# Sparse attention's score masks: from matrix products on the tensor engine to the vector engine's pass over the scores

## The chip, the cores and the metric

The kernel runs on one core of a Trainium2 chip. The metric is the device time of one launch in microseconds (us). The core has a tensor engine (PE; its weight loads are listed apart as PEld), a vector engine (DVE), a scalar engine (ACT), GpSimd (POOL) and a sync engine (SP) whose queue issues the DMAs here. Each engine takes its own instructions in order and waits for others by semaphores. Matrix products read SBUF and write PSUM; DVE and ACT read both.

## The reference, cut to what matters

The program is one decoder layer of 1024 tokens and width 1024: a common input projection, sparse attention with three branches (compressed, selected, window), gated linear attention, a gated merge, an output projection and a feed-forward block. The change touches the selected and the window branch. There are 2 key groups with 4 heads each, a head dimension of 64, and 8 query blocks of 128 tokens. With 16 selected blocks of 64 keys out of 16, the selected branch covers all earlier keys; the window is 512 wide.

```
sw = einsum('bghqd,bgkd->bghqk', q_pos, kwin)
m_w = (kpos >= 0) & (dist >= 0) & (dist < WINDOW)
p_w = softmax(where(m_w, sw, -1e30)) * m_w
o_w = einsum('bghqk,bgkd->bghqd', p_w, vwin)
```

So of the key blocks that one query block looks at, the last one (the diagonal) needs a lower triangle as its mask, and in a full window the first one (the edge) needs the opposite triangle. All the blocks between are unmasked.

## The kernel before

**Stages.** The input projection and the compressed keys come first, then gated linear attention (to about 340 us), then sparse attention (about 366 to 763 us), the merge, the output projection, and the feed-forward block. Products in full precision are made of three products of rounded 32-bit parts: lines L427, L1483 to L1485 and L1871 to L1873.

**Attention's units.** A unit is a group g and a query block i: `units` runs through (0, 7) down to (0, 0) and then (1, 0) up to (1, 7). A unit has five branches: the compressed one (`br` 0), and the selected (`br` 1) and the window one (`br` 2) for each of two head pairs j. A branch that looks at `nkb` key blocks has scores of w = 128 * nkb columns for each of its two heads. Up to four key blocks both heads share one score tile and one pass ("pair", `pair_scores`, query blocks 0 to 3, 32 passes in all). With more, each head has its own ("head", `head_scores`, query blocks 4 to 7, 64 passes in all; 40 of them 640 wide).

**One pass.** `products` puts the scores into a PSUM tile s (two such tiles exist): for each part of at most 512 columns a product with the high part of the queries (L1122) and one with the low part (L1123). Then masks are added by products with a 16-bit identity as weights: `meb` for the edge (L1125, when br is 2 and i is at least 4) and `mdb` for the diagonal (L1127, always). DVE reduces the scores to their negated maximum nm (L1150 for a pair, L1163 for a head), ACT computes exp(s + nm) from PSUM into a tile p in SBUF and sums it into z (L1153, L1165; the sum is read out by a second instruction), DVE inverts z (L1133), and the two heads are scaled, one on DVE (L1141), the other on ACT (L1139). Then p is transposed on PE (L1201), split into two parts (ACT L1178, DVE L1179) and multiplied with the values (L1210). There are four p buffers.

**What sets the order.** PE's order is the program's. `Plan` walks through the scores, the transposes ("turns") and the value products with estimated costs for PE, DVE, ACT and POOL, and wherever the next of these is over 300 ns away it issues one dense product from a queue named `fill` (14 gate and 5 up projections, L427, into the PSUM tile d). What is left of the queue after the last branch is flushed there. `score_at` gives no scores for a branch before the p buffer that they will use has been given back, and `turn` gives it back after the last transposes of its branch. The other engines' orders come from the framework's scheduler. SP issues all loads and stores in the order in which they stand in its queue.

**The queries' rooms.** Gated linear attention uses two constant tiles `QZ` (name qz, 128 x 512 values of 32 bits), in which the two heads' queries lie in halves padded with zeros. They are filled by L833, read by PE (L870) and by DVE (L849), and unused once its last chunk is done.

**Constants.** One array `consts` holds the identity, the masks and others by column; `load_consts` copies `mdb` and `meb` to 16-bit tiles at the start, from one load of 768 columns.

Of the kernel before, what the change touches and what calls it, by code (L numbers as in the profile page):

```python
# [12 lines left out]
BF = mybir.dt.bfloat16  # L13
U8 = mybir.dt.uint8
AF = mybir.ActivationFunctionType
OP = mybir.AluOpType
# [14 lines left out]

CI, CTRI, CMD, CME, CCMP, CMUL, CLEV = 0, 128, 256, 384, 512, 1024, 1088
NCONST = CLEV + 64 * NLV


def constants():
    c = np.zeros((128, NCONST), np.float32)
    r = np.arange(128)[:, None]  # L40
    j = np.arange(128)[None, :]
    c[:, CI:CI + 128] = r == j
    c[:, CTRI:CTRI + 128] = (r <= j) / 16.0
    c[:, CMD:CMD + 128] = np.where(j <= r, 0.0, NEG)
    c[:, CME:CME + 128] = np.where(j > r, 0.0, NEG)
    n = np.arange(64)[None, None, :]
    t = np.arange(NB)[None, :, None] * 128 + np.arange(128)[:, None, None]
    ok = (n * CSTRIDE + CLEN - 1 <= t) & (n < NCMP)
    c[:, CCMP:CCMP + 512] = np.where(ok, 0.0, NEG).reshape(128, 512)
    c[:, CMUL:CMUL + 64] = ok[:, 0]  # L50
    for i, h in enumerate(LEVELS):
        q = np.arange(64)[None, :]
        c[:, CLEV + 64 * i:CLEV + 64 * (i + 1)] = (r // (2 * h) == q // h) & (r % (2 * h) < h)
    return c


def rope_tables():
# [51 lines left out]
class Plan:  # L109
# [52 lines left out]
    def score(self):  # L162
        b, fn, n = self.scores.popleft()
        fn()
        w = 64 if b.br == 0 else 128 * b.nkb
        if b.br == 0:
            cost = 540.0
        else:
            cost = n * (2 * max(107.0, w / 2.4) + 55.0 * (1 + (b.br == 2 and b.i >= 4)))
        self.t += cost  # L170
        self.s.pop(0)
        pf = self.p.pop(0) if b.br else 0.0
        m = n if b.br else 4
        t = self.on("D", self.t, 65 + 1.041 * w * m)
        t = self.on("A", max(t, pf), m * (237 + 0.833 * w))
        self.s.append(t + LAT)
        self.s.sort()
        t = self.on("D", t, 150.0)
        t = max(self.on("D", t, 130 + 0.52 * w if b.br else 330.0), self.on("A", t, 187 + 0.833 * w) if b.br and n == 2 else 0.0)
        b.ready = max(b.ready or 0.0, t + LAT)  # L180
        b.left = getattr(b, "left", 2) - n
# [58 lines left out]
def layer_kernel(ctx, tc, a, outT):  # L240
# [79 lines left out]
    onesr = cst.tile([128, 128], F32R, name="onesr")  # L320
    meanr = mcst.tile([128, 128], F32R, name="meanr")
    identb = mcst.tile([128, 128], BF, name="identb")
    mdb = mcst.tile([128, 128], BF, name="mdb")
    meb = mcst.tile([128, 128], BF, name="meb")
    cmb = mcst.tile([128, NB, 64], BF, name="cmb")
    lev = mcst.tile([128, NLV, 64], U8, name="lev")
    gains = cst.tile([128, 3, NK], F32, name="gains")
# [4 lines left out]
    def load_consts():  # L332
        load(ident, a["consts"][:, CI:CI + 128])
        load(tri, a["consts"][:, CTRI:CTRI + 128])
        load(cmul, a["consts"][:, CMUL:CMUL + 64])
        load(ggain, a["gla_norm"])
        load(w2b, a["gla_w2b"])
        V.tensor_copy(identb, ident)
        t = big("cst1")
        load(t[:, :768], a["consts"][:, CMD:CMD + 768])  # L340
        V.tensor_copy(mdb, t[:, 0:128])
        V.tensor_copy(meb, t[:, 128:256])
        V.tensor_copy(cmb.rearrange("p b n -> p (b n)"), t[:, 256:768])
        t = big("cst2")
        load(t[:, :64 * NLV], a["consts"][:, CLEV:CLEV + 64 * NLV])
        V.tensor_copy(lev.rearrange("p b n -> p (b n)"), t[:, :64 * NLV])
# [684 lines left out]


    psum("pp2", s=2, t=2, o=1, d=1)
    oa = [[None, None], [None, None]]
    spare = deque([ps_d])

# [39 lines left out]
    class Branch:  # L1076
# [37 lines left out]
        def products(self, par, s, w, parts):  # L1114
            d = UN[self.g, self.i]
            kk = ks[self.br - 1][self.g]
            edge = self.br == 2 and self.i >= 4
            for o, n in parts:
                dst = s[:, o:o + n]
                kv = kk[:, 128 * self.k0 + o:128 * self.k0 + o + n]  # L1120
                end = o + n == w
                PE.matmul(dst, d["qs"][par][:, 0, self.j, :], kv, start=True, stop=False)  # L1122
                PE.matmul(dst, d["qs"][par][:, 1, self.j, :], kv, start=False, stop=not end and not (edge and o == 0))  # L1123
                if edge and o == 0:
                    PE.matmul(s[:, 0:128], identb, meb, start=False, stop=not end)  # L1125
                if end:
                    PE.matmul(s[:, w - 128:w], identb, mdb, start=False, stop=True)  # L1127

        def weigh(self, pars, ps, z):

# [12 lines left out]
        def pair_scores(self):  # L1143
# [3 lines left out]
            for par in range(2):  # L1147
                self.products(par, s[:, par, :], w, [(0, w)])
            nm, z = tiny("nm", 2, 6), tiny("z", 2, 6)
            V.tensor_reduce(nm, s, AX, OP.max, negate=True)  # L1150
            p = prob("p", shape=(2, 512))[:, :, :w]
            for par in range(2):
                S.activation(p[:, par, :], s[:, par, :], AF.Exp, bias=nm[:, par:par + 1],  # L1153
                             accum_out=z[:, par:par + 1])
            self.weigh((0, 1), [p[:, 0, :], p[:, 1, :]], z)

        def head_scores(self, par):
# [2 lines left out]
            s = ps_s()[:, 512 - c:512 - c + w]  # L1160
            self.products(par, s, w, [(0, c), (c, w - c)][:1 if c == w else 2])
            nm, z = tiny("nm", 2, 6)[:, :1], tiny("z", 2, 6)[:, :1]
            V.tensor_reduce(nm, s, AX, OP.max, negate=True)  # L1163
            p = prob("p")[:, :w]
            S.activation(p, s, AF.Exp, bias=nm, accum_out=z)  # L1165
            self.weigh((par,), [p], z)

        def turns(self):
# [773 lines left out]
```

## Time and profile before

| what | value |
|---|---|
| median of 3 runs | 1574.86 us (1574.77 to 1575.18) |
| span of the profiled execution | 1571.8 us |
| median less the span | 3.1 us |
| instructions | 23022 |
| sparse attention, by its score passes | 366 to 756 us |
| diagonal mask products (L1127), edge mask products (L1125) | 128, 32 |
| granted TensorE clock, mean | 0.999 |

The profiled execution's own time is not listed beside its span; what lies around the span is taken as 3.1 us, the distance to the median. A row of the timeline gives an instruction's start, its duration, engine, line, and what it writes and reads. Products overlap on PE, and their ends are modelled, so durations on PE add up to more than the time they take: what a product costs is read from the distance between starts. "Busy" in the table of stretches is the union of the durations.

### The profile page before, as it was taken

The numbers are of one execution on the slowest core, as the hardware profiler recorded it, in microseconds if no ns is written. First come the engines' busy times: TensorE is split into PE (matmuls) and PEld (weight loads), VectorE is DVE, ScalarE is ACT, GpSimd is POOL, SyncE is SP. The second block draws the span as 40 slices with busy tenths as digits, with TensorE's granted clock in tenths as the row PEclk, the third lists the DMA queues.
The fourth block names the chain that finished last, engine by engine and source line by source line (L and its number), as shares of the span: only waits on it lengthen the run. The fifth ranks groups of instructions, "written<-read, shape, count | busy, mean of one in ns | idle before, by whom it ended". The sixth has DMA issues, their size and how long they took to land.

```text
span 1571.8 us, 23022 instructions
## 1 busy us (share of the span) xinstructions
PE 1556.8 (99%) x8031; PEld 1310.1 (83%) x8031; DVE 1014.1 (65%) x1630; ACT 810.0 (52%) x1615; POOL 719.7 (46%) x635
## 2 busy tenths in 40 slices
PE   9999999999999999999999999999999999999998
PEld 7888988888888888888888888888888888888887
DVE  7780487686777687667574577644444444499785
ACT  6241555575676686677654454334433334454542
POOL 6110466563223353253256520666666666555570
PEclk9999999999999999999999999999999999999999
DMA  5431112232111221131656622323222222795422
GB/s 180 140 104 62 61 55 79 97 107 81 45 51 57 71 83 56 51 109 60 205 184 211 215 83 81 114 101 106 102 101 101 101 101 101 282 340 161 141 88 107
DMA packets 109656, 179.86 MB, mean 114 GB/s; under 512 B 13394, under 2 KB 30435, under 8 KB 109540
## 3 DMA queue, kind: packets, MB, share of 16 engines
q1 hardware_dynamic: 105508, 171.96, 32.5%
q10 hardware_dynamic: 4032, 6.44, 1.1%
q8 instruction: 63, 1.03, 0.3%
q14 instruction: 53, 0.43, 0.1%
HBM read 128.27 MB, written 45.88 MB: 111 GB/s over the span
## 4 chain that ended last, share of the span: by engine, by line
PE 93%; DVE 4%; ACT 1%; issue 1%; DMA 1%; POOL 0%; SPq 0%; DVEq 0%; ACTq 0%; POOLq 0%
PE m L427 19%; PE d L427 10%; PE m L1484 9%; PE m L1485 9%; PE m L1483 9%; PE m L1873 4%; PE m L1871 4%; PE m L1872 4%; PE o L1210 4%; PE t L1201 3%; PE s L1122 2%; PE s L1123 2%; PE t L745 2%; PE t L747 1%; PE t L746 1%; PE t L880 1%
## 5 line engine op out<-in xcount | busy, mean ns | idle before, releaser
L369 POOL TENSOR_TENSOR wl<-wf,wh 128x512 fp32r<-128x512 f32 x106 | 146.3, 1385 | 275.6 <-ACT wh L368 274.8
L1484 PE MATMUL m<-xt,wh 128*128 128x512 f32 x412 | 160.3, 389 | 0.0
L1483 PE MATMUL m<-xt,wh 128*128 128x512 f32 x412 | 160.3, 389 | 0.0
L1485 PE MATMUL m<-xt,wl 128*128 128x512 f32 x412 | 160.3, 389 | 0.0
L1400 POOL TENSOR_TENSOR wl<-ws,wh 128x512 fp32r<-128x512 f32 x76 | 107.5, 1419 | 73.6 <-ACT wh L1399 73.6
L1400 POOL TENSOR_TENSOR wl<-wr,wh 128x512 fp32r<-128x512 f32 x69 | 92.0, 1333 | 70.0 <-ACT wh L1399 70.0
L1179 DVE TENSOR_TENSOR ptl<-t,pth 128x512 fp32r<-128x512 f32 (+1 forms) x168 | 99.5, 596 | 34.4 <-ACT pth L1178 31.4
L1399 ACT ACTIVATE wh<-wr 128x512 fp32r<-128x512 f32 x87 | 55.0, 632 | 121.0 <-POOL wl L1400 90.4
L1399 ACT ACTIVATE wh<-ws 128x512 fp32r<-128x512 f32 x76 | 48.0, 632 | 131.7 <-PE m L1484 112.6
L1178 ACT ACTIVATE pth<-t 128x512 fp32r<-128x512 f32 (+1 forms) x168 | 87.8, 524 | 53.2 <-PE t L1201 45.5
L1871 PE MATMUL m<-xb,wh 128*128 128x512 f32 x280 | 109.1, 389 | 0.3 <-DVE g L1545 0.3
L1400 POOL TENSOR_TENSOR wl<-wd,wh 128x512 fp32r<-128x512 f32 x56 | 82.1, 1468 | 58.9 <-ACT wh L1399 58.7
L1872 PE MATMUL m<-xb,wh 128*128 128x512 f32 x280 | 109.0, 389 | 0.0
L1873 PE MATMUL m<-xb,wl 128*128 128x512 f32 x280 | 108.9, 389 | 0.0
L1400 DVE TENSOR_TENSOR xb<-ar,xb 128x512 fp32r<-128x512 f32 x73 | 82.5, 1150 | 28.8 <-ACT xb L1399 28.8
L368 ACT ACTIVATE wh<-wf 128x512 fp32r<-128x512 f32 x106 | 66.2, 627 | 67.5 <-PE m L427 19.7
L427 PE MATMUL m<-hh,wh 128*128 128x512 f32 x240 | 99.9, 416 | 0.0
L427 PE MATMUL m<-hh,wl 128*128 128x512 f32 x240 | 93.8, 391 | 0.0
L427 PE MATMUL m<-hl,wh 128*128 128x512 f32 x240 | 93.6, 390 | 0.0
L1483 PEld LDWEIGHTS m<-xt,wh 128*128 128x128 f32 x412 | 77.4, 188 | 16.2
L1484 PEld LDWEIGHTS m<-xt,wh 128*128 128x128 f32 x412 | 77.4, 188 | 16.0
L1485 PEld LDWEIGHTS m<-xt,wl 128*128 128x128 f32 x412 | 77.4, 188 | 16.0
(422 smaller groups left out, 4569.4 us busy)
## 6 DMA issues: line engine op xcount, KB each, us to landing
ar<-actd SPq DMA_DIRECT2D x77, 256.0 KB, 3.0
wf<-in_w_t SPq DMA_DIRECT2D x58, 256.0 KB, 2.7
wr<-in_w_gate SPq DMA_DIRECT2D x44, 256.0 KB, 2.7
wr<-in_w_upf SPq DMA_DIRECT2D x44, 256.0 KB, 2.6
wd<-in_w_down SPq DMA_DIRECT2D x33, 256.0 KB, 5.1
zd<-zt SPq DMA_DIRECT2D x32, 256.0 KB, 2.0
zz<-zd SPq DMA_DIRECT2D x16, 512.0 KB, 4.6
wf<-in_w_out SPq DMA_DIRECT2D x32, 256.0 KB, 3.3
```

The costliest lines, as they stand in the source:

```text
L369: P.tensor_tensor(tl, wf, f(th), OP.subtract)
L427: PE.matmul(st["p"], w, x, start=k + i == 0, stop=k == n - 1 and i == 2)
L1178: S.activation(th[:, :c], pt[:, :c], AF.Copy)
L1179: V.tensor_tensor(tl[:, :c], pt[:, :c], f(th[:, :c]), OP.subtract)
L1399: S.activation(th, src, AF.Copy)
L1400: eng.tensor_tensor(tl, src, f(th), OP.subtract)
L1483: PE.matmul(ps, wh[:, c], xh, start=first and k == 0, stop=False, skip_group_check=not first)
L1484: PE.matmul(ps, wh[:, c], xl, start=False, stop=False, skip_group_check=not first)
L1485: PE.matmul(ps, wl[:, c], xh, start=False, stop=k == MH - 1, skip_group_check=not first)
L1871: PE.matmul(dst, wh[:, c], xh, start=first and p == 0, stop=False, skip_group_check=not first)
L1872: PE.matmul(dst, wh[:, c], xl, start=False, stop=False, skip_group_check=not first)
L1873: PE.matmul(dst, wl[:, c], xh, start=False, stop=p == NP - 1, skip_group_check=not first)
```

## The change

The two mask products and their weight loads go. In their place DVE's pass over the scores adds a mask from SBUF while it reads the scores from PSUM, writes -(s + mask) to the tile p, and reduces it by a minimum, which gives the negated maximum as before. ACT then computes exp(-p + nm) in place in p, from SBUF in place of PSUM. The mask of a pass is as wide as its scores: 1024 columns of 16 bits with the diagonal triangle at the end (the last w of them are used), and 640 columns with both triangles for the full windows. They are loaded into the two `QZ` tiles, packed two values to a 32-bit word, after gated linear attention. A pair's pass becomes two, one for each head. In `Plan`, a mask no longer counts on PE, the DVE pass has 65 ns for each head in place of each pass and waits for the p buffer, and the score tile comes free after DVE's pass in place of ACT's.

```diff
-CI, CTRI, CMD, CME, CCMP, CMUL, CLEV = 0, 128, 256, 384, 512, 1024, 1088
-NCONST = CLEV + 64 * NLV
+CI, CTRI, CCMP, CMUL, CLEV = 0, 128, 256, 768, 832
+CMS = CLEV + 64 * NLV
+CMW = CMS + 512
+NCONST = CMW + 320
...
+    late, edge = np.where(j <= r, 0.0, NEG), np.where(j > r, 0.0, NEG)
+    c[:, CMS:CMS + 512] = halves(np.concatenate([np.zeros((128, 896)), late], 1))
+    c[:, CMW:CMW + 320] = halves(np.concatenate([edge, np.zeros((128, 384)), late], 1))
...
-            cost = n * (2 * max(107.0, w / 2.4) + 55.0 * (1 + (b.br == 2 and b.i >= 4)))
+            cost = n * 2 * max(107.0, w / 2.4)
...
-        t = self.on("D", self.t, 65 + 1.041 * w * m)
-        t = self.on("A", max(t, pf), m * (237 + 0.833 * w))
-        self.s.append(t + LAT)
+        t = self.on("D", max(self.t, pf), 65 * m + 1.041 * w * m)
+        u, t = t, self.on("A", t, m * (237 + 0.833 * w))
+        self.s.append((u if b.br else t) + LAT)
...
-        load(t[:, :768], a["consts"][:, CMD:CMD + 768])
-        V.tensor_copy(mdb, t[:, 0:128])
-        V.tensor_copy(meb, t[:, 128:256])
-        V.tensor_copy(cmb.rearrange("p b n -> p (b n)"), t[:, 256:768])
+        load(t[:, :512], a["consts"][:, CCMP:CCMP + 512])
+        V.tensor_copy(cmb.rearrange("p b n -> p (b n)"), t[:, :512])
...
     psum("pp2", s=2, t=2, o=1, d=1)
+    masks = []
+    for t, o, n in zip(QZ, (CMS, CMW), (512, 320)):
+        t = t.rearrange("p a b c -> p (a b c)")[:, :n]
+        SP.dma_start(t, a["consts"][:, o:o + n])
+        masks.append(t.bitcast(BF))
...
-                PE.matmul(dst, d["qs"][par][:, 1, self.j, :], kv, start=False, stop=not end and not (edge and o == 0))
-                if edge and o == 0:
-                    PE.matmul(s[:, 0:128], identb, meb, start=False, stop=not end)
-                if end:
-                    PE.matmul(s[:, w - 128:w], identb, mdb, start=False, stop=True)
+                PE.matmul(dst, d["qs"][par][:, 1, self.j, :], kv, start=False, stop=True)
+
+        def masked(self, p, s, w, nm):
+
+            m = masks[1] if self.br == 2 and self.i >= 4 else masks[0][:, 1024 - w:]
+            V.tensor_tensor_reduce(out=p, in0=s, in1=m, scale=-1.0, scalar=3.0e38, op0=OP.add, op1=OP.min, accum_out=nm)
...
             nm, z = tiny("nm", 2, 6), tiny("z", 2, 6)
-            V.tensor_reduce(nm, s, AX, OP.max, negate=True)
             p = prob("p", shape=(2, 512))[:, :, :w]
             for par in range(2):
-                S.activation(p[:, par, :], s[:, par, :], AF.Exp, bias=nm[:, par:par + 1],
+                self.masked(p[:, par, :], s[:, par, :], w, nm[:, par:par + 1])
+            for par in range(2):
+                S.activation(p[:, par, :], p[:, par, :], AF.Exp, scale=-1.0, bias=nm[:, par:par + 1],
                              accum_out=z[:, par:par + 1])
...
-            V.tensor_reduce(nm, s, AX, OP.max, negate=True)
             p = prob("p")[:, :w]
-            S.activation(p, s, AF.Exp, bias=nm, accum_out=z)
+            self.masked(p, s, w, nm)
+            S.activation(p, p, AF.Exp, scale=-1.0, bias=nm, accum_out=z)
```

Line numbers shift: L1122 and L1123 become L1129 and L1130, L1150 and L1163 become L1135, L427 becomes L431, L1201 and L1210 become L1210 and L1219, L1179 becomes L1188.

**PE, a head of a full window** (the first one, of unit (0, 7)): what stood there before, from the scores' first part to the next dense product:

```order
L1122 MATMUL s<-ks_920,qs 128x384
L1123 MATMUL s<-ks_920,qs 128x384
L1125 LDWEIGHTS identb
L1125 MATMUL s<-meb,identb 128x128
L1122 MATMUL s<-ks_920,qs 128x256
L1123 MATMUL s<-ks_920,qs 128x256
L1127 LDWEIGHTS identb
L1127 MATMUL s<-mdb,identb 128x128
L427 MATMUL d<-hl,wh 128x512
```

And the same head in the change:

```order
L1129 MATMUL s<-ks_916,qs 128x384
L1130 MATMUL s<-ks_916,qs 128x384
L1129 MATMUL s<-ks_916,qs 128x256
L1130 MATMUL s<-ks_916,qs 128x256
L431 MATMUL d<-hh,wl 128x512
```

Both masks and their loads of weights are gone, and the score products follow each other directly. In the whole program 160 such products go. Of these, 148 stood ahead of another rounded 32-bit product (L427, L1122, L1193, L1210), 12 ahead of a transpose (L1185, L1201).

**DVE, the pairs of unit (0, 3)** (512 columns for each head), before:

```order
L1179 TENSOR_TENSOR ptl<-t,pth 128x256
L1150 TENSOR_REDUCE nm<-s 128x2
L1179 TENSOR_TENSOR ptl<-t,pth 128x512
L1150 TENSOR_REDUCE nm<-s 128x2
L1133 RECIPROCAL rr<-z 128x2
```

And in the change, where qz is the mask in the queries' room:

```order
L1188 TENSOR_TENSOR ptl<-t,pth 128x256
L1135 ISA p,nm<-s,qz_1345 128x512
L1135 ISA nm 128x1
L1135 ISA p,nm<-s,qz_1345 128x512
L1135 ISA nm 128x1
L1188 TENSOR_TENSOR ptl<-t,pth 128x512
L1135 ISA p,nm<-s,qz_1345 128x512
L1135 ISA nm 128x1
L1135 ISA p,nm<-s,qz_1345 128x512
L1135 ISA nm 128x1
L1141 RECIPROCAL rr<-z 128x2
```

One reduction of a pair becomes four instructions: for each head the pass and a second instruction that writes out its minimum. A head's reduction becomes two.

**PE, the end of attention** (after the last value products), before:

```order
L1210 MATMUL o<-ptl,vs_1043 128x256
L1210 MATMUL o<-ptl,vs_1044 128x256
L1210 MATMUL o<-pth,vs_1044 128x256
L1210 MATMUL o<-ptl,vs_1044 128x256
L427 MATMUL t<-obh,wh 128x512
L427 MATMUL t<-obl,wh 128x512
L427 MATMUL t<-obh,wl 128x512
```

And in the change:

```order
L1219 MATMUL o<-ptl,vs_1039 128x256
L1219 MATMUL o<-ptl,vs_1040 128x256
L1219 MATMUL o<-pth,vs_1040 128x256
L1219 MATMUL o<-ptl,vs_1040 128x256
L431 MATMUL m<-obh,wh 128x512
L431 MATMUL m<-obl,wh 128x512
L431 MATMUL m<-obh,wl 128x512
```

Before, 36 dense products of the fill queue (12 into t, 12 into o, 12 into d) stood between the last value product and the merge's first product (into m). In the change none do: all of the queue is issued within attention. The largest move is between the compressed scores of unit (0, 0) and those of unit (1, 3) (L1102 before, L1111 in the change): 94 dense products stood there before, and 142 do in the change.

More of the change, by code (lines that the diff above doesn't have):

```diff
@@ L43, in constants @@
     c[:, CTRI:CTRI + 128] = (r <= j) / 16.0
-    c[:, CMD:CMD + 128] = np.where(j <= r, 0.0, NEG)
-    c[:, CME:CME + 128] = np.where(j > r, 0.0, NEG)
     n = np.arange(64)[None, None, :]
@@ L53, in constants, with halves @@
         c[:, CLEV + 64 * i:CLEV + 64 * (i + 1)] = (r // (2 * h) == q // h) & (r % (2 * h) < h)
-    return c
+    late, edge = np.where(j <= r, 0.0, NEG), np.where(j > r, 0.0, NEG)
+    c[:, CMS:CMS + 512] = halves(np.concatenate([np.zeros((128, 896)), late], 1))
+    c[:, CMW:CMW + 320] = halves(np.concatenate([edge, np.zeros((128, 384)), late], 1))
+    return c
+def halves(m):
+    bits = np.ascontiguousarray(m, np.float32).view(np.uint32) >> 16
+    return (bits[:, 0::2] | (bits[:, 1::2] << 16)).astype(np.uint32).view(np.float32)
 def rope_tables():
@@ L322, in layer_kernel @@
     identb = mcst.tile([128, 128], BF, name="identb")
-    mdb = mcst.tile([128, 128], BF, name="mdb")
-    meb = mcst.tile([128, 128], BF, name="meb")
     cmb = mcst.tile([128, NB, 64], BF, name="cmb")
@@ L1116, in products @@
             kk = ks[self.br - 1][self.g]
-            edge = self.br == 2 and self.i >= 4
             for o, n in parts:
@@ L1120, in products @@
                 kv = kk[:, 128 * self.k0 + o:128 * self.k0 + o + n]
-                end = o + n == w
                 PE.matmul(dst, d["qs"][par][:, 0, self.j, :], kv, start=True, stop=False)
-                PE.matmul(dst, d["qs"][par][:, 1, self.j, :], kv, start=False, stop=not end and not (edge and o == 0))
-                if edge and o == 0:
-                    PE.matmul(s[:, 0:128], identb, meb, start=False, stop=not end)
-                if end:
-                    PE.matmul(s[:, w - 128:w], identb, mdb, start=False, stop=True)
+                PE.matmul(dst, d["qs"][par][:, 1, self.j, :], kv, start=False, stop=True)
+        def masked(self, p, s, w, nm):
+            m = masks[1] if self.br == 2 and self.i >= 4 else masks[0][:, 1024 - w:]
+            V.tensor_tensor_reduce(out=p, in0=s, in1=m, scale=-1.0, scalar=3.0e38, op0=OP.add, op1=OP.min, accum_out=nm)
         def weigh(self, pars, ps, z):
```

## The prediction

> **What bounds the kernel now.** First the page's head, then its chain of work that ended last.
>
> ```profile
> span 1571.8 us, 23022 instructions
> PE 1556.8 (99%) x8031; PEld 1310.1 (83%) x8031; DVE 1014.1 (65%) x1630; ACT 810.0 (52%) x1615; POOL 719.7 (46%) x635
> PE 93%; DVE 4%; ACT 1%; issue 1%; DMA 1%; POOL 0%; SPq 0%; DVEq 0%; ACTq 0%; POOLq 0%
> ```
>
> PE is busy all the time and holds 93% of the chain, so work taken from PE shortens the program unless another engine then makes PE wait. The change lies in attention only, so next the table of stretches for all of attention and for the stretch in which its score passes are shortest (units (0, 1) to (1, 2)). The columns are PE, PEld, DVE, ACT and POOL busy, with counts, then clock and DMA.
>
> ```profile
> 366.00:756.00 390.00, 387.12 (x2458) 330.57 (x2457) 285.56 (x645) 272.59 (x679) 131.81 (x134) 1.00 0.20 65
> 541.00:598.00 57.00, 55.80 (x380) 48.46 (x379) 47.24 (x136) 44.19 (x154) 25.95 (x28) 1.00 0.23 70
> ```
>
> In attention PE lacks 2.9 us of work in 390. DVE is busy for 73% of it, and for 83% in the narrow stretch. There the chain passes through DVE, in rows like these:
>
> ```profile
> 589.05 0.60 DVE ptl L1179
> 589.65 0.87 DVE nm L1150
> ```
>
> So attention is PE's, with one place of some tens of us in which DVE is as late as PE.
>
> **The masks on PE: minus 19.3 us.** A mask's own row says 0.23 us, but the distance between starts tells the price. PE's timeline, at the end of the first unit's first head scores and at the first head of a full window:
>
> ```profile
> 368.94 0.40 PE L1123 MATMUL s<-ks,qs 128*128 128x512 f32 x1
> 369.17 0.23 PE L1127 MATMUL s<-mdb,identb 128*128 128x128 bf16 x1
> 369.21 0.48 PE L427 MATMUL d<-hh,wh 128*128 128x512 f32 x1
> 369.53 0.39 PE L427 MATMUL d<-hl,wh 128*128 128x512 f32 x1
> 369.76 0.40 PE L427 MATMUL d<-hh,wl 128*128 128x512 f32 x1
> ...
> 371.27 0.23 PE L1125 MATMUL s<-meb,identb 128*128 128x128 bf16 x1
> 371.31 0.36 PE L1122 MATMUL s<-ks,qs 128*128 128x256 f32 x1
> 371.51 0.28 PE L1123 MATMUL s<-ks,qs 128*128 128x256 f32 x1
> 371.63 0.23 PE L1127 MATMUL s<-mdb,identb 128*128 128x128 bf16 x1
> ```
>
> Products of 512 columns start 0.23 apart (369.53 to 369.76). The mask at 369.17 is followed after 0.04, but the product behind it takes 0.32 until the next: 0.04 + 0.32 - 0.23 = 0.13 us for a mask. At 256 columns: 0.04 from 371.27 to 371.31, then 0.20 to 371.51 where the next one takes 0.12 (to 371.63): also 0.12. I take 0.125. A mask ahead of transposes costs less:
>
> ```profile
> 367.26 0.39 PE L1123 MATMUL s<-ks,qs 128*128 128x512 f32 x1
> 367.49 0.39 PE L1122 MATMUL s<-ks,qs 128*128 128x512 f32 x1
> 367.72 0.39 PE L1123 MATMUL s<-ks,qs 128*128 128x512 f32 x1
> 367.95 0.23 PE L1127 MATMUL s<-mdb,identb 128*128 128x128 bf16 x1
> 368.01 0.39 PE L1185 MATMUL t<-ident,ec 128*128 128x128 f32 x2
> ```
>
> The mask at 367.95 is followed after 0.06; I take 0.07. The counts are those of the two groups:
>
> ```profile
> L1127 PE MATMUL s<-mdb,identb x128: 229/230/233, 367.9 to 752.7; 128*128 128x128 bf16 x128
> L1125 PE MATMUL s<-meb,identb x32: 229/230/231, 371.3 to 752.4; 128*128 128x128 bf16 x32
> ```
>
> By the order 148 of these 160 stand ahead of a rounded product and 12 ahead of a transpose: 148 x 0.125 + 12 x 0.07 = 19.3 us. With 0.12 and 0.13 for all of the 148, the ends are 18.6 and 20.1. Nothing covers them now, since PE hardly waits, so their whole price is on the path.
>
> [...]
>
> **DVE's pass: plus 25 us of DVE, nothing of it on the path outside the narrow stretch.** The trace shows no pass that adds and reduces at once. Nearest are the plain reductions and the subtraction that reads PSUM and SBUF and writes SBUF (L1179), and for the readout of the minimum a one-column DVE instruction:
>
> ```profile
> L1163 DVE TENSOR_REDUCE nm<-s 128x1 f32<-128x640 f32 x40 | 32.2, 818 | 8.1 <-PE s L1127 8.0
> L1150 DVE TENSOR_REDUCE nm<-s 128x2 f32<-128x1024 f32 x8 | 9.7, 1220 | 0.7 <-PE s L1127 0.7
> L1179 DVE TENSOR_TENSOR ptl<-t,pth 128x512 fp32r<-128x512 f32 x107 | 73.3, 686 | 29.6 <-ACT pth L1178 27.1 <-issue 0.5
> L1133 DVE RECIPROCAL rr<-z 128x1 f32<-128x1 f32 x64 | 10.1, 159 | 4.9 <-ACT p L1165 3.9
> ```
>
> A reduction of 1024 takes 1.22 us and one of 640 takes 0.818: 0.402 for 384 columns, 1.05 ns each, and 0.15 fixed. L1179 at 512 columns is 0.686, the same line. So I take the new pass at the reduction's price, and 0.159 for the readout. A head then costs 0.159 more. A pair costs 2 x 0.686 - 1.22 = 0.152 more for its second pass, and two readouts: 0.47. Together 64 x 0.159 + 32 x 0.47 = 25.2 us. From below the readout could be free: 32 x 0.152 = 4.9 us. From above the pass streams at half speed; that is a rival.
>
> DVE has the room: 285.6 + 25.2 = 311 in 390 - 19 = 371 us, 84%. In the narrow stretch stand 18 pairs (four each of the units (0, 0) and (1, 0) to (1, 2), and two of (0, 1)): 47.2 + 18 x 0.47 = 55.7 of DVE, while PE loses 36 masks there, 4.5 us of its 57. That would be over 100%, were it not that 48 more dense products stand there in the change: 48 x 0.228 = 10.9 us, with two more DVE evacuations of 0.69. So 57.1 of DVE in 63.4 us, 90% where it was 83%. Those products are the 36 that stood at attention's end and some from other units, so they cost PE nothing in sum. For PE's waits there, 1.2 us now, I put in **plus 2 us**. The bounds: 0, since the cover grows; 8.5, if all of the 18 x 0.47 ends up on the path.
>
> **ACT from SBUF.** The exponential reads p in place of s. The nearest rows, of 640 columns from PSUM and from SBUF:
>
> ```profile
> L1165 ACT ACTIVATE p<-s,nm 128x640 f32<-128x640 f32 x40 | 31.7, 794 | 16.4 <-DVE nm L1163 16.2
> L1139 ACT ACTIVATE p<-p,rr 128x640 f32<-128x640 f32 x20 | 16.5, 827 | 0.8 <-DVE rr L1138 0.7
> ```
>
> 0.033 more for each of 128, 4.2 us of ACT, which is busy for 273 of 390. The score tile comes free about one exponential sooner, which helps PE; a pair's first exponential can start after half of the pair's columns, so its chain gets no longer. A head's chain gets longer by the readout. Nothing on the path.
>
> **Waits that are added or moved.** The pass now writes p, so DVE waits for p's last reader, the transposes two branches back, and whatever is queued on DVE behind it (L1179's splits, on which value products wait) would wait too. But scores are planned only after those transposes, and PE runs in order, so they are done when the scores are: the wait ends with the scores, as now ("PE s L1127" in the rows above). The masks' loads wait on SP until the rooms are free:
>
> ```profile
> 269.76 0.38 SPq L827 DMA_DIRECT2D vc<-vgd  x1
> 271.23 1.08 DVE L849 TENSOR_TENSOR xq<-xx,qz 128x256 f32<-128x256 f32 x3
> 282.71 1.99 DVE L849 TENSOR_TENSOR xq<-xx,qz 128x256 f32<-128x256 f32 x3
> 284.85 0.57 SPq L897 DMA_DIRECT2D obd<-ot  x1
> ```
>
> The first stands in SP's queue right ahead of the last vc load and holds it from 269.8 to about 272.3; that chunk's values are multiplied around 291. The second waits until 284.7, and the store behind it goes at 284.85 anyway. First use is at 368. No cost. Two casts of 128 columns and a third of one load at the start go; off the path, nothing.
>
> **The end of attention.** With no dense products left, what is late next is the merge's wait for the last unit's output:
>
> ```profile
> 763.29 0.38 PE L1210 MATMUL o<-ptl,vs 128*128 128x256 f32 x1
> 765.88 1.29 DVE L1288 TENSOR_TENSOR oal<-oa,oah 128x512 fp32r<-128x512 f32 x2 [0.70 <-ACT oah L1285]
> 771.67 0.39 PE L427 MATMUL m<-obh,wh 128*128 128x512 f32 x1
> 774.39 0.39 PE L427 MATMUL m<-oah,wh 128*128 128x512 f32 x1
> ```
>
> The last split ends at 767.2, 3.9 us after the last value product starts. The merge begins with 12 products that need only obh (771.67 to 774.39, 2.7 us) and 6 more of the other group's oah (1.4 us), 4.1 us in all. Just covered: 0, at most 1.3 if all of oah waits.
>
> **Sum.** 1571.8 - 19.3 + 2.0 = 1554.5 for the span, and with 3.1 around it **1557.6 us**, against the median of 1574.86: 1.1% faster. [...] The likeliest case's own range is 1554 (20.1 saved, no waits) to 1565 (18.6 saved, 8.5 given back).
>
> **Rivals.**
> 1. *Readouts and second passes fall on the path.* The narrow stretch speaks for it (the chain passes through L1150 there), the 48 dense products against. With a readout of 0.3 a pair costs 0.75 more, and 32 pairs give 24 x half on the path, 12 us: 1574.9 - 19.3 + 12 = about 1568; range 1565 to 1571.7.
> 2. *The pass streams at half speed,* on the other side. The two groups of reductions hold 57.8 and 26.1 us:
>
> ```profile
> L1163 DVE TENSOR_REDUCE nm<-s 128x1 f32<-128x640 f32 (+3 forms) x64 | 57.8, 918 | 9.0 <-PE s L1127 8.9
> L1150 DVE TENSOR_REDUCE nm<-s 128x2 f32<-128x1024 f32 (+3 forms) x32 | 26.1, 817 | 3.1 <-PE s L1127 2.9
> ```
>
> Less 96 x 0.15 fixed, 69 us are columns, and would be paid twice: 311 + 69 = 380 us of DVE, more than PE's 371. At the 90% of a crowded stretch that takes 422 us in place of 390, so about 1600. It decides from about 334 us of DVE (90% of 371), which is 1.4 ns a column. Against it: L1179 reads PSUM and SBUF and writes at 1.05 ns a column. [...]
> 3. *The slow start behind a mask stays,* as a mark of a score group's end. Then only 0.04 of each mask goes, 6.4 us, and the time is about 1570. Against it: L1122 follows L1123 without a mask at 367.49, the start of the next part, and the next product comes after the usual 0.23 (367.72).
> 4. *More than the masks is won,* since score tiles come free sooner: at most the 2.9 us that PE lacks in attention, about 1553.
>
> **Chances.** Forecast (1554 to 1565) 0.63; rival 1 0.16; rival 2 0.08; rival 3 0.04; rival 4 0.04; no measurable change, the waits eating all, 0.05. The range 1553 to 1572 holds the forecast, rivals 1, 3 and 4. A measurement tells about 0.2% from no change, 3.1 us; faster by more 0.86, within 0.05, slower 0.09.
>
> **What would show it.** Right: no L1125 and L1127; products in attention 0.23 apart at 512 columns everywhere; PE's busy time in attention about 19 us less, DVE's 25 more, the pass of 640 columns near 0.82 and its readout near 0.16; PE's lack of work in attention under 6 us; the merge's first product with oah without a wait. Wrong: a pass of 640 columns at 1.4 us, or DVE as the releaser of PE's waits for over 8 us between units (0, 1) and (1, 3), or a load of qz that ends after 366.

## The result, and the profile after

| what | before | after |
|---|---|---|
| median of 4 runs of each, side by side | 1575.02 us (1574.77 to 1575.58) | 1566.99 us (1563.62 to 1570.1) |
| ratio to before, 95% interval | | 0.9941 (0.9928 to 0.9955) |
| span of the profiled execution; its own time | 1571.8; not listed | 1563.0; 1564.79 |
| from the last product of attention's first compressed scores (L1102, after L1111) to the merge's first product | 361.44 to 771.67, 410.2 us | 361.99 to 762.12, 400.1 us |

The change won 8.0 us by the medians, 8.8 by the two spans, where 17.3 were forecast. 1.8 us lie around the span after, not the 3.1 that the prediction took.

The page's head and its chain, after:

```profile
span 1563.0 us, 22871 instructions
PE 1542.0 (99%) x7871; PEld 1309.6 (84%) x7871; DVE 1014.2 (65%) x1788; ACT 813.0 (52%) x1615; POOL 720.4 (46%) x635
PE 93%; DVE 3%; ACT 1%; issue 1%; POOL 0%; DVEq 0%; POOLq 0%; ACTq 0%
```

These shares hardly moved, so they say nothing of what came back. The table of stretches does, for the whole of attention, first before and then after (PE, PEld, DVE, ACT, POOL busy, then clock and DMA):

```profile
361.40:771.70 410.30, 407.31 (x2567) 347.73 (x2567) 294.51 (x664) 282.08 (x702) 136.98 (x140) 1.00 0.23 75
```

```profile
362.00:762.10 400.10, 391.44 (x2406) 346.78 (x2404) 293.27 (x820) 286.81 (x702) 138.48 (x141) 1.00 0.23 74
```

PE is 15.9 us less busy, but the stretch is only 10.2 shorter: PE lacked work for 3.0 us before and for 8.7 after. The list of PE's waits says at whose hands (us in total, times, longest), before and after:

```profile
PE t L1201 <- DVE ptl L1179: 1.0, 2, 0.7
PE t L1185 <- DVE ptl L1179: 0.8, 1, 0.8
PE s L1099 <- ACT p L1153: 0.4, 1, 0.4
PE o L1193 <- DVE fp L1227: 0.3, 1, 0.3
```

```profile
PE t L1210 <- DVE ptl L1188: 6.1, 10, 2.7
PE t L1210 <- ACT p L1147: 1.4, 1, 1.4
PE t L1210 <- DVE rr L1141: 0.7, 2, 0.4
PE d L431 <- DVE zt L969: 0.2, 1, 0.2
```

PE's transposes wait for a free tile t, which DVE's split L1188 empties. The longest wait, 2.7 us, stands at attention's end; the other nine share 3.4 us.

**A finer account.** Busy time on PE rests on modelled ends, so for the comparisons below every product of this stretch is priced by the distance between starts that it has when nothing disturbs it (512 columns 0.228 us, 384 0.174, 256 0.118, 128 0.059, the unrounded products of the compressed scores 0.112, transposes 0.109 or 0.028, 16-bit masks 0.03 to 0.07, 0.084 more for the first rounded product behind a transpose or a 16-bit mask). What a distance exceeds that by, from 0.02 us on, is counted as a wait.

| kernel | stretch | products | waits | of these after 750 us |
|---|---|---|---|---|
| before | 410.2 | 400.5 | 7.1 | 0.8 |
| after | 400.1 | 381.4 | 16.3 | 4.5 |

So the products lost 19.0 us, where 19.3 were forecast, and 9.2 us of waits came: 3.8 at the end of attention and 5.4 inside it. The slower products of a stretch at half clock (757.70 to 761.20 us below) count as waits too. (The remainder, 2.6 and 2.4 us, is in distances under the bound.) Ahead of and behind the stretch the profile after is 0.55 and 0.75 us longer.

**The end of attention, after.** A row of the timeline gives start, duration, engine, line; in brackets the idle time ahead of it and its releaser:

```profile
752.51 0.63 ACT L372 ACTIVATE wh<-wf 128x512 fp32r<-128x512 f32 x1 [0.46 <-PE d L431]
753.16 1.28 ACT L1344 ACT_TABLE_LOAD   x1
754.46 1.06 ACT L1344 ACTIVATE zz<-zz 128x1024 f32<-128x1024 f32 x1
755.42 0.58 ACT L1255 ACTIVATE zt<-d 128x512 f32<-128x512 f32 x1
755.90 1.07 ACT L1187 ACTIVATE pth<-t 128x512 fp32r<-128x512 f32 x2
756.52 1.29 DVE L1188 TENSOR_TENSOR ptl<-t,pth 128x512 fp32r<-128x512 f32 x2 [4.79 <-ACT pth L1187]
757.27 0.70 PE L1210 MATMUL t<-ident,p 128*128 128x128 f32 x4 [2.73 <-DVE ptl L1188]
```

The list of waits names DVE, but DVE itself was idle for 4.79 us: ACT had the merge's first sigmoid (L1344), its table load and another evacuation in its queue ahead of attention's last splits. And then the clock:

```profile
753.00:757.70 4.70, 1.97 (x19) 1.76 (x17) 1.18 (x2) 3.94 (x6) 1.28 (x1) 1.00 0.55 152
757.70:761.20 3.50, 3.50 (x20) 3.50 (x18) 1.49 (x3) 1.39 (x3) 0.00 (x0) 0.51 0.98 364
761.20:765.00 3.80, 3.80 (x22) 3.31 (x22) 1.76 (x4) 1.93 (x4) 0.00 (x0) 1.00 0.86 267
```

The granted clock is 0.51 for the 3.5 us behind the wait. The merge's sigmoid is kept in program order on ACT, behind the last weight split of the dense products (L372, 752.51). Before, 36 dense products were left over at the end, so that split came after attention's splits; in the change the planner uses all of them inside, and it comes ahead.

**Inside attention, after.** A place where PE waits for a split while DVE makes two passes in a row:

```profile
405.46 0.81 DVE L1135 CUSTOM_DVE_ANT_0 p<-s,qz 128x640 f32<-128x640 f32 x1
405.77 0.36 ACT L1187 ACTIVATE pth<-t 128x256 fp32r<-128x256 f32 x1
406.20 0.08 DVE L1135 DVE_READ_ACCUMULATOR2_ANT nm<- 128x1 f32 x1
406.20 0.82 DVE L1135 CUSTOM_DVE_ANT_0 p<-s,qz 128x640 f32<-128x640 f32 x1
406.95 0.75 DVE L1188 TENSOR_TENSOR ptl<-t,pth 128x256 fp32r<-128x256 f32 x2
407.51 0.63 PE L1210 MATMUL t<-ident,p 128*128 128x128 f32 x4 [0.44 <-DVE ptl L1188]
```

ACT's half of the split is done at 406.13, DVE's half starts at 406.95 behind the second pass. DVE's rows overlap, as PE's do: the readout and the next pass both start at 406.20, 0.74 us after the first pass.

### The profile page after: what moved, and what is told of

Same layout as the page of the kernel before. It is cut to its first block, busy times and chain, and to the rows that moved or that the text cites. A ratio compares the mean times of both kernels' runs of the same rounds, so it can differ in the third digit from the quotient of the medians.

```text
span 1563.0 us, 22871 instructions
## 1 busy us (share of the span) xinstructions
PE 1542.0 (99%) x7871; PEld 1309.6 (84%) x7871; DVE 1014.2 (65%) x1788; ACT 813.0 (52%) x1615; POOL 720.4 (46%) x635
## 4 chain that ended last, share of the span: by engine, by line
PE 93%; DVE 3%; ACT 1%; issue 1%; POOL 0%; DVEq 0%; POOLq 0%; ACTq 0%
PE m L431 19%; PE d L431 11%; PE m L1494 9%; PE m L1492 9%; PE m L1493 9%; PE m L1880 5%; PE m L1882 4%; PE m L1881 4%; PE t L1210 3%; PE o L1219 3%; PE s L1130 2%; PE s L1129 2%; PE t L749 2%; PE t L750 1%; PE t L751 1%; PE t L884 1%
## 5 line engine op out<-in xcount | busy, mean ns | idle before, releaser
L1188 DVE TENSOR_TENSOR ptl<-t,pth 128x512 fp32r<-128x512 f32 (+1 forms) x168 | 99.2, 597 | 42.7 <-ACT pth L1187 40.5
L431 PE MATMUL m<-hh,wh 128*128 128x512 f32 x240 | 99.9, 416 | 0.1
L372 ACT ACTIVATE wh<-wf 128x512 fp32r<-128x512 f32 x106 | 66.1, 626 | 61.1 <-PE m L431 19.9
L1135 DVE CUSTOM_DVE_ANT_0 p<-s,qz 128x640 f32<-128x640 f32 (+7 forms) x128 | 86.3, 700 | 12.8 <-PE s L1130 12.5
L431 PE MATMUL m<-hh,wl 128*128 128x512 f32 x240 | 93.8, 391 | 0.0
L431 PE MATMUL m<-hl,wh 128*128 128x512 f32 x240 | 93.6, 390 | 0.0
L1210 PE MATMUL t<-ident,p 128*128 128x128 f32 x528 | 83.9, 275 | 8.4 <-DVE ptl L1188 6.1
L1493 PEld LDWEIGHTS m<-xt,wh 128*128 128x128 f32 x412 | 77.4, 188 | 16.2
```

What stands on the lines that cost most here:

```text
L431: PE.matmul(st["p"], w, x, start=k + i == 0, stop=k == n - 1 and i == 2)
L1188: V.tensor_tensor(tl[:, :c], pt[:, :c], f(th[:, :c]), OP.subtract)
L1210: PE.transpose(pt[:, bs(2 * b + par)], self.p[par][:, bs(kb + b)], ident)
L1493: PE.matmul(ps, wh[:, c], xl, start=False, stop=False, skip_group_check=not first)
```

## The experiments

Three questions: does the end cost what the rows above suggest; do the waits inside come from the new pass, from the planner's prices, or from work that stood close behind PE all along; and can they be won back? In each, the kernel before was timed on the same chip.

**The masks alone.** The kernel before without its mask products, so its scores are unmasked. All other instructions stay, and PE's stay in their order; the scheduler of the framework orders DVE's and ACT's anew, and another instruction stands in 143 of DVE's 1630 places and in 171 of ACT's 1615.

```diff
-                PE.matmul(dst, ..., kv, start=False, stop=not end and not (edge and o == 0))
-                if edge and o == 0:
-                    PE.matmul(s[:, 0:128], identb, meb, start=False, stop=not end)
-                if end:
-                    PE.matmul(s[:, w - 128:w], identb, mdb, start=False, stop=True)
+                PE.matmul(dst, ..., kv, start=False, stop=True)
```

> The kernel before with nothing taken out but the 160 mask products (the scores stay unmasked; planner, reduction and exponential as before). Main theory: the products' price is the 19.0 us that the distances between starts give, and the new pass and the planner gave part of it back. Then this runs at 1575.0 - 19.0 + 0 to 3 us of new waits: 1556 to 1559. Rival, the masks were worth only what the change won (8 us): 1565 to 1568.

Measured: 1564.66 us (1562.21 to 1567.81), ratio 0.9936 (0.9917 to 0.9954). The stretch is 398.1 us, products 381.5, waits 14.2, of them 0.4 after 750. With all of DVE's and ACT's old instructions, 19.0 us less of products on PE shorten the stretch by 12.1 us and the program by 11.3, less than the theory's 16 to 19 and just over the rival's gain: 7.5 us more of waits than before stand ahead of 750, about half of them between 493 and 598 us.

**The planner's prices undone.** The change with the costs of before in `Plan` (55 ns for each mask on PE, one DVE pass of 65 + 1.041 w for a pair, the score tile free after ACT); 36 dense products are then left over at the end again.

> The change with the planner's costs of before, so that PE's order is that of before without the masks, and 36 dense products stand at attention's end again. Main theory (3.8 us lost at attention's end to the merge's first sigmoid on ACT, about 5.4 inside attention to DVE's pass): the end's loss goes, the inner one stays: 1559 to 1562. Rival, the planner's new order makes the inner waits too: 1556 to 1558. Rival, all of it is the pass: 1566 to 1568.

Measured: 1563.57 us (1563.08 to 1564.33), ratio 0.9923 (0.9908 to 0.9937). Waits 13.3, 0.5 after 750: the end is repaired, the waits inside stay, 12.8 us against the change's 11.8.

**The sigmoid last.** The change, with the merge's first sigmoid queued on ACT behind attention's last split; PE and DVE keep their orders row for row.

```diff
-    masks = []
+    masks, ends = [], []
...
-            S.activation(th[:, :c], pt[:, :c], AF.Copy)
+            ends[:] = [S.activation(th[:, :c], pt[:, :c], AF.Copy)]
...
-                    tc.keep_in_program_order(S.activation(zz, zz, AF.Sigmoid))
+                    if ends:
+                        with tc.issue_after(ends.pop().ins):
+                            S.activation(zz, zz, AF.Sigmoid)
+                    else:
+                        tc.keep_in_program_order(S.activation(zz, zz, AF.Sigmoid))
```

> The change with the merge's first sigmoid and its table load queued on ACT behind the last split of attention; PE's and DVE's orders are those of the change. Main theory: PE's wait of 2.9 us at attention's end and the half clock after it (about 2 us more) go: 1560 to 1562.5, and the runs lie within 1 us of each other where the change's lie within 6.5. Rival, that wait is paid elsewhere if it goes (the table load then delays the last unit's output): 1565 to 1568.

Measured: 1561.28 us (1560.5 to 1564.45), ratio 0.9911 (0.9897 to 0.9926). Stretch 396.5, waits 12.6, 1.0 after 750: 3.7 us less waiting than the change and 3.6 us less in the stretch, 4.7 us by the two ratios. The same transposes now, and the table load behind them:

```profile
754.09 0.66 PE L1210 MATMUL t<-ident,p 128*128 128x128 f32 x4 [0.37 <-DVE ptl L1188]
757.03 1.28 ACT L1346 ACT_TABLE_LOAD   x1
```

```profile
750.00:757.70 7.70, 7.31 (x53) 6.49 (x52) 3.99 (x9) 5.31 (x10) 1.29 (x1) 1.00 0.62 200
```

PE waits 0.37 us there, and the clock stays at 1.00. The cost of the end is shown. That the four runs would lie within 1 us of each other did not come true: the slowest is 3.1 us above the next. All versions below but the next keep this edit or the end of before.

**The old pass.** The change's planner and PE order, but DVE's plain reduction and ACT's exponential from PSUM as before; the scores are unmasked.

> The change's planner and PE order with the reduction and exponential of before (scores unmasked, no mask products). The sigmoid still stands ahead of the last splits on ACT. Theory that the inner waits are DVE's pass (readout, second pass, exponential from SBUF): about 5 us less than the change, 1561 to 1563. Rival, the inner waits come of PE being faster than DVE's order allows whatever the pass is: within 2 us of the change, 1565 to 1568.

Measured: 1568.73 us (1565.06 to 1570.8), ratio 0.9952 (0.9936 to 0.9968). Waits 18.4, 4.9 after 750. The waits inside, 13.5 us against 11.8, are there without the new pass, so it doesn't make them. (In this version the old exponential holds the score tile for longer than the planner counts on; PE's waits for such a tile come to 1.6 us in its list of waits, which leaves 11.9.)

**The planner's prices changed.** Three versions on top of the one with the sigmoid last: DVE's price for a head's pass from 65 + 1.041 w to 240 + 1.041 w ns (first); all of DVE's and ACT's prices in attention raised to the rows' durations (second); 70 ns less on PE for each former mask (third).

> The change with the sigmoid last (as c_sigmoid_last), and with the planner's price of DVE's pass raised from 65 to 240 ns for each head (measured: 0.15 fixed and 0.08 for the readout). The masks' removal left the waits inside attention 5 to 7 us longer whatever the pass was. Theory P, the planner places products by too low prices of DVE and ACT, and the masks' own time that it did not count (0.125 against 55 ns) had covered that: waits inside attention fall from 11.7 us to 8 or 9, 1557.5 to 1559.5. Rival Q, DVE and ACT are simply the limit where PE is faster, and no placement helps: within 1.5 us of c_sigmoid_last, 1560 to 1562.5.

> As h1_plan_pass, with the planner's other prices of DVE and ACT raised to the measured ones too (exponential with its readout, inversion, scaling, splits). Theory P: waits inside attention at 6 to 8 us, 1556 to 1558.5, unless the dense products run out before the last unit, which they do in this order (none stands in the last unit): that part then costs a few us more. Rival Q: 1560 to 1563.

> As c_sigmoid_last, with the planner's PE time of a score group lowered by 70 ns for each mask that it once had, which is what the planner left out of a mask's price before. Theory P in its narrow form (that error was the cover): waits inside attention fall to about 7 us, 1556 to 1558. Rival Q, or the order hardly changes: 1560 to 1562.5.

Measured: 1568.11 us (1567.27 to 1570.5), 1580.04 (1577.94 to 1583.91) and 1565.88 (1564.34 to 1567.51), ratios 0.995, 1.0024 and 0.9933; waits 19.6, 31.3 and 16.6 against 12.6. All three lost time. In the second the planner sees its engines fuller and spends the dense products sooner, until none is left for the last unit: 16.9 us of waits lie between 598 and 750 us there. The raised prices were not better ones, though: rows overlap, and by the distance between starts DVE's old price was nearly right, 65 + 1.041 x 640 = 731 ns against the 0.74 us from 405.46 to 406.20 in the change. So a price of DVE's pass that was too low doesn't make the waits, and no version here tests a better set of prices than the old one.

**More work on DVE.** The version with the sigmoid last, with one small DVE operation behind each of the 128 passes; PE's order is the same.

```diff
+    spill = tiny("spill", 64)
...
+            tc.keep_in_program_order(V.tensor_scalar(spill, identb[:, 0:64], 1.0, None, op0=OP.mult))
```

> As c_sigmoid_last, with one more small DVE instruction behind each of the 128 passes (64 columns, about 0.1 us, read by nobody): 13 to 19 us more DVE work, PE's order unchanged. If attention's waits are those for DVE's queue (Q), a good part shows: 3 us or more, 1564 to 1568. If DVE has room and only single placements are late (P), under 2 us: 1560.5 to 1563.

Measured: 1573.03 us (1571.0 to 1575.07), ratio 0.9981 (0.9972 to 0.999). Stretch 406.3, waits 22.4. DVE's busy time in the stretch against that of the version with the sigmoid last, and PE's list of waits:

```profile
365.00:771.30 406.30, 391.50 (x2406) 345.40 (x2404) 319.84 (x948) 286.65 (x701) 138.55 (x141) 1.00 0.22 70
```

```profile
361.30:757.70 396.40, 390.20 (x2406) 345.23 (x2404) 292.65 (x820) 285.19 (x701) 139.03 (x141) 1.00 0.23 72
```

```profile
PE t L1212 <- DVE ptl L1190: 6.9, 12, 2.0
PE t L1212 <- ACT p L1149: 2.4, 2, 2.0
PE t L1212 <- DVE spill L1137: 2.4, 3, 1.3
```

27.2 us more on DVE cost 9.8 us in the stretch: 0.36 us for each, though DVE is busy for only 79% of it. The time is above both forecasts.

**The same on the kernel before.** Mask products in place, and the same number of such operations behind DVE's reductions.

> The kernel before with 128 small operations more on VectorE, one for each head's maximum, as in the run that lost 11.8 us with the change. Its 160 mask products stand, so TensorE is 19 us slower through the same attention. Theory (the mask products' time on TensorE covered VectorE's queue): it loses less than half of that, 2 to 6 us, 1577 to 1581. Rival (VectorE's price is on the path at the same rate with or without the mask products): 10 to 13 us, 1585 to 1588.

Measured: 1582.97 us (1581.15 to 1585.73) against 1576.99, ratio 1.004 (1.0026 to 1.0053): 6.0 us lost, at the edge of the theory's 2 to 6. Stretch 416.4, waits 13.3:

```profile
363.30:779.70 416.40, 408.83 (x2566) 348.99 (x2566) 315.31 (x792) 282.91 (x702) 137.07 (x140) 1.00 0.23 74
```

DVE has 20.8 us more here, and the stretch is 6.1 us longer: 0.29 for each. But about 3.4 of the 6.1 come from one place. At 561 us PE's longest wait for a split is 2.5 us, where it was 0.8 before, and behind it the granted clock is 0.50 for 3.4 us, which by an estimate takes half of that, 1.7 us:

```profile
564.40:567.80 3.40, 3.40 (x15) 2.94 (x14) 2.64 (x14) 1.97 (x7) 0.00 (x0) 0.50 0.55 195
```

The stretch of the version above, with such work added and no mask products, has no such half clock. Without that place 2.7 us are left, 0.13 for each. So the masks covered some of DVE's work; how much, one traced execution of each doesn't say.

**Less work on DVE.** The version with the sigmoid last, where the 64 products of a head's reciprocal with its gate are made by GpSimd (first) or by ACT (second).

```diff
-                    V.tensor_mul(ri, ri, gi)
+                    P.tensor_tensor(ri, ri, gi, OP.mult)
```

```diff
-                    V.tensor_mul(ri, ri, gi)
+                    S.activation(ri, ri, AF.Copy, scale=gi)
```

> The version with the sigmoid queued last, and 64 of VectorE's operations less: the product of a head's reciprocal with its gate (L1146, 64 of 245 ns, 15.7 us) is made by GpSimd. TensorE's order is the same row for row. Theory (VectorE's queue is on the path, at the 0.45 to 0.5 us for each us that the added operations cost): 7 us are won, 1553 to 1557 against 1561.3. Rival (the queue is only sensitive to more work, not to less, since TensorE's other waits stand right behind): 1559 to 1563. Second rival: the 128x1 product stands behind a weight split of 1.4 us on GpSimd, ScalarE waits for it with its whole queue: 1563 or more.

> As the run beside it, but the 64 products of reciprocal and gate are made by ScalarE, right ahead of the scaling that uses them: VectorE has 15.7 us less, ScalarE about 13 us more (64 of some 0.2 us). TensorE's order is the same. Theory that VectorE's queue alone is on the path: 1553 to 1557. Theory that the two queues stand equally close behind TensorE: the gain is given back, 1559 to 1563. That ScalarE's stands closer: 1564 or more.

Measured: 1562.38 us (1561.18 to 1564.98), ratio 0.9909 (0.9893 to 0.9925), and 1558.08 us (1556.83 to 1560.11), ratio 0.9877 (0.986 to 0.9893), both against 1576.99. Waits 12.5 and 9.1, against 12.6. The stretches, first and second, then PE's waits with the sigmoid last alone and in the second:

```profile
365.40:761.80 396.40, 389.92 (x2406) 345.45 (x2406) 284.56 (x756) 285.47 (x701) 150.46 (x205) 1.00 0.23 72
```

```profile
365.10:758.10 393.00, 389.29 (x2407) 345.32 (x2407) 284.52 (x756) 296.88 (x765) 138.78 (x141) 1.00 0.23 73
```

```profile
PE t L1210 <- DVE ptl L1188: 3.7, 10, 0.6
PE t L1210 <- ACT p L1147: 1.3, 1, 1.3
```

```profile
PE t L1210 <- DVE ptl L1188: 2.7, 7, 0.6
PE o L1202 <- DVE fp L1236: 0.4, 1, 0.4
PE t L1210 <- DVE rr L1141: 0.3, 1, 0.3
```

DVE is relieved of the same 8.1 us in both. On ACT that wins 3.5 us of the stretch, though ACT has 11.7 more; on GpSimd it wins nothing, and the list of waits of the first shows where ACT's queue stands then:

```profile
ACT p L1147 <- POOL rr L1146: 5.8, 12, 1.0
```

With the sigmoid last alone, ACT waited 7.4 us for the same product from DVE. In the second version the product is ACT's own, and it waits 2.8 us, for the reciprocal. So DVE's busy time is not the whole of it: what counts is when the splits queued on DVE and ACT come through, and an ACT that stands and waits holds them too. Which of the two made the 3.5 us isn't separated; 1.3 of them are one wait, for ACT's scaling (L1147), that the second version's list no longer has.

**The same relief on the kernel before.** Mask products in place, the 64 products on ACT.

> The kernel before, its mask products kept, with the 64 products of reciprocal and gate moved from VectorE to ScalarE, which won some 3 to 5 us where the mask products were gone (ratio 0.9877 against 0.9911; 396.5 to 392.9 us from the first compressed scores to the merge). TensorE's order is that of before. Theory (the mask products' time covers VectorE's queue, so that its relief is worth little there): at most 1.5 us, 1573.5 to 1575.5 where before stands at 1575, and 409 to 410.5 us for that stretch. Rival (the relief is worth the same with and without the mask products): 3 to 5 us, 1570 to 1572, and 406 to 407.

Measured: 1574.61 us (1571.77 to 1575.71) against 1576.44, ratio 0.9981 (0.9972 to 0.999). Stretch 407.4, waits 4.3:

```profile
366.00:773.40 407.40, 406.31 (x2567) 347.49 (x2565) 283.65 (x600) 293.81 (x766) 136.33 (x140) 1.00 0.23 75
```

That stretch is 2.8 us shorter than before, with 10.9 us less on DVE and 11.7 more on ACT, between the theory's 0 to 1.5 and the rival's 3 to 5. The theory that the masks' time *covers* the queues as long as it stands, and that they are bare without it, is too sharp.

The rates together, in us of the stretch for a us of DVE's busy time: without the masks 0.36 for work added, 0.43 for work moved to ACT and 0 for work moved to GpSimd; with them 0.29 for work added (0.13 without the one place at half clock) and 0.26 for work moved to ACT. And of the 19 us taken from PE alone, with the same instructions on the other engines, 6.9 us, 0.36 for each, came back. Each of these is one traced execution, and a few waits of 1 to 3 us make up much of each, so they are no constant. What they agree on is that DVE's and ACT's queues stand close behind PE through most of attention: the waits ahead of 750 us are 6.3 us before, and 11.6 to 13.8 in each of the five versions without mask products whose planner has the prices of before or of the change (the masks alone, the old prices, the change, the sigmoid last, the old pass). Whether another order of these two queues would win the waits back wasn't tried.

## Why the prediction was right in part

The measured 1566.99 us lies within the wide range of 1553 to 1572, but above the 1554 to 1565 of the forecast itself, and about half of the forecast gain came. The wide range reaches that far because it also takes in rivals 1 and 3. Neither of their mechanisms is what happened, so it is luck in part that the range holds the result. Of the signs named for right, PE's lack of work in attention (8.7 us, not under 6) and the 25 us more of DVE failed.

- **The masks on PE, minus 19.3 us: right.** The products of the stretch lost 19.0. Behind the first full window's scores the next products start at undisturbed distances:

```profile
370.11 0.34 PE L1129 MATMUL s<-ks,qs 128*128 128x384 f32 x1
370.29 0.34 PE L1130 MATMUL s<-ks,qs 128*128 128x384 f32 x1
370.46 0.28 PE L1129 MATMUL s<-ks,qs 128*128 128x256 f32 x1
370.58 0.28 PE L1130 MATMUL s<-ks,qs 128*128 128x256 f32 x1
370.70 0.39 PE L431 MATMUL d<-hh,wl 128*128 128x512 f32 x1
370.93 0.39 PE L431 MATMUL d<-hh,wh 128*128 128x512 f32 x1
```

  Rival 3 (the slow start stays) is out: the dense product behind the scores takes 0.23 (370.70 to 370.93), where the one behind the mask took 0.32 before.
- **"Nothing covers them now, since PE hardly waits, so their whole price is on the path": the step that failed.** PE hardly waited, but that shows only that it was last most of the time, not by how much. The run with the masks alone gave 11 us, not 19, with the same instructions on the other engines: some 7 us of new waits came in the stretch, most of them for DVE's splits and reciprocals (3.4 and 2.2 us in its list of waits). What was mis-sized is the share of the masks' price that reaches the path, about 12 us in place of 19.3. Rival 4 looked at the same place from the other side: the one wait for a score tile in the list of before, 0.4 us, is gone after.
- **DVE's pass, plus 25 us: almost nothing, and not what cost the time.** Groups of DVE's instructions, after:

```profile
L1135 DVE CUSTOM_DVE_ANT_0 p<-s,qz 128x640 f32<-128x640 f32 (+7 forms) x128 | 86.3, 700 | 12.8 <-PE s L1130 12.5
```

```profile
L1135 DVE CUSTOM_DVE_ANT_0 p<-s,qz 128x640 f32<-128x640 f32 x40 | 31.8, 817 | 7.2 <-PE s L1130 7.1
L1135 DVE DVE_READ_ACCUMULATOR2_ANT nm<- 128x1 f32 x128 | 10.4, 82 | 0.0
```

  The pass over 640 columns takes 0.817 us, the reduction's price (0.818). The readout takes 0.082, not 0.159. By these durations passes and readouts are 86.3 + 10.4 = 96.7 us against 83.9 before, 12.8 more in place of 25.2. But that sum, like the prediction's, adds up rows that overlap. In the table of stretches DVE is busy for 293.3 us after and 294.5 before. By starts a pass of 640 with its readout takes 0.74 us (405.46 to 406.20 above), and so did the reduction before:

```profile
371.90 0.82 DVE L1163 TENSOR_REDUCE nm<-s 128x1 f32<-128x640 f32 x1
372.64 0.15 DVE L1133 RECIPROCAL rr<-z 128x1 f32<-128x1 f32 x1
```

  Of a pair, two passes of 512 columns take about 1.21 us by starts and the one reduction took 1.13. Over all passes that is about 3 us more. The half speed of rival 2 is out: no run shows it, and the 0.817 stands where the prediction named 1.4 as its sign.
- **Plus 2 us in the narrow stretch: 0, but waits elsewhere.** Between 493 and 598 us the waits are 2.6 us, 3.0 before; the dense products that moved there cover it, as was argued. The waits came in the wide units, where the table of stretches looked roomy: 4.2 us ahead of 493 (0.7 before) and 5.0 between 598 and 750 (2.7 before), where units of 4 and more key blocks stand for the most part. Rival 1's time, 1568, is the nearest to the median, but its place and its cause were others. (Between 493 and 598 us the run with the masks alone, whose dense products had not moved, waits for 6.9 us.)
- **ACT from SBUF:** 0.824 us in place of 0.794 for 640 columns, where 0.827 was taken. **The loads on SP:** issued at 273.0 and 285.4 us, as early as was said.
- **"Just covered: 0, at most 1.3" at the end of attention: wrong by 3.8 us.** The wait that it weighed, oah's, didn't come: the merge's first product with oah starts 0.23 behind its forerunner. But with no dense products left, something else was late: the merge's own sigmoid, queued on ACT ahead of the last splits, with 2.73 us of wait and 3.5 us at half clock behind it. The step looked at what the merge waits for and not at what the merge puts in ACT's queue.

Put right, the sum is 1571.8 - 19.0 + 5.4 + 3.8, less 0.2 in distances under the bound and plus 1.3 outside the stretch: 1563.1 us, against the span of 1563.0. The time that was forecast, 1.1% less, is about what the version with the sigmoid last and the gate's products on ACT reaches (ratio 0.9877). Three figures of the prediction are off by a little: rival 3 comes to 1568.5 us by its own 6.4 (1570 is said), rival 2 to 1607 (1600), and the lower end of the forecast to 1554.8 (1554).

Not settled is why two of the change's four runs were 4 to 5 us longer than the profiled one; there is no trace of them. The other traces show one thing that can do this, in a part where all kernels are the same: in four of them, among them the second version with less work on DVE, the clock is halved for 3.4 us in the input projection (0.50 from 70.5 to 73.9 us there), and attention begins at 365.0 to 366.0 us, where it begins at 361.3 to 363.8 in the others. So by where attention begins whole times can differ by 1 to 5 us, and the stretches are the better comparison.

## What to carry to other kernels

An engine that is busy for 99% can have others right behind it: before its work is counted as a gain, ask how long each instruction that feeds it was done before it was needed, and take only part of the price if that is short; here some two thirds came through when the mask products alone went. Price work by the distance between starts on every engine: a row's duration can overlap the next row's, on DVE (a row of 0.81 us at 405.46, the next pass 0.74 behind its start) as on PE (a row of 0.39 at 370.70, the next 0.23 behind its start). Idle time of the other engines in a table of stretches doesn't show this, since what stands ahead in a queue holds all that is behind it: here the merge's sigmoid with its table load stood ahead of attention's last splits on ACT, and DVE was idle for 4.79 us and PE for 2.73. And where filler work is used up sooner, look at what the next stage puts into each queue at that point: a sigmoid and its table load that came early cost about 4 us here.

## What the runs showed of the hardware

- A wait of PE of 2.73 us was followed by 3.5 us at a granted clock of 0.51; so it was in the version with the old pass (0.52), with the same 3.0 us between two products' starts. Behind 2.0 us between starts (507.2 us in the run with the masks alone taken out) the clock stayed at 1.00:

```profile
509.00:512.50 3.50, 3.24 (x20) 2.99 (x20) 2.89 (x7) 1.97 (x5) 0.00 (x0) 1.00 0.41 122
```

  The length of a single wait did not tell the two apart in these traces: 2.41 us between starts at 512.4 us in the version with more work on DVE left the clock at 1.00, and in the version with all prices raised 2.41 us at 754.4 were followed by 3.4 us at 0.50, and so were 1.62 us at 729.0 (with 0.94 at 727.1 ahead of them).
- DVE's pass that adds, scales, writes and reduces at once, from PSUM and a 16-bit tile, costs as much as a plain reduction (0.817 and 0.818 us for 640 columns; 0.74 us each from its start to the start of the work behind it). Its readout's row is 0.082 us long, but the next pass starts with it (406.20 us), so it adds next to nothing. ACT's readout of a sum has a row of 0.188 us.
